# Window attention in three parts a step, values in two passes, and accumulating transfers for the low parts of weights

## The chip, the cores and the metric

The kernel runs on one core of a Trainium2 chip. The metric is the device time of one execution in microseconds (us); the number reported is the median of several runs. The engines are TensorE (PE; its weight loads are PEld), VectorE (DVE), ScalarE (ACT), GpSimd (POOL) and SyncE (SP, which issues the transfers). L172 is line 172 of the kernel before.

## The reference

Two layers of a hybrid block on a sequence of 512 tokens of width 1024 (a convolution branch, a retention branch and a window attention branch, each gated, summed and projected), and then one layer of a second block (a spatial gate, a gated linear recurrence, a feed-forward part). All in float32. What the change touches is the window attention of the first block, run once in each of the two layers:

```
q, k, v = h @ w_in (16 heads of 64; 4 key/value heads of 64, each used by 4 heads)
q, k    = rms_norm over 64, rotary on 16 of the 64
for each block n of 128 queries: keys of blocks n-1, n, n+1 (2 blocks at the ends)
    s = q k^T / 8, masked to |i - j| <= 128
    m = max(max(s), sink);  p = exp(s - m) / (sum(exp(s - m)) + exp(sink - m))
    o = p v
y_attn = (o * silu(gate)) @ w_attn_out
```

## The kernel before, in words

**Products in three passes.** A float32 product is made of three passes of TensorE over operands split into a high part (rounded to the format fp32r) and a low part (the value less its high part): high x high, high x low, low x high (`mm3`, L170 to L174). `fm` makes one 128 x 512 product tile from 8 blocks of weights of 128 x 128, so 24 passes of 512 columns, in one of two PSUM banks of the pool `mm`. `tm` makes four tiles at a time in the four banks of the pool `acc`. A third pool, `misc`, has two banks.

**Weights.** All weights come as chunks of 8 blocks (128 x 1024, 512 KB) in the order of their use. SP loads a chunk into one of three `raw` tiles; `_split_next` (L132) makes `hi` on ACT (L149) and `lo = raw - hi` on DVE (L150), in three tiles each (WB = 3). `take` (L155) splits chunk c + 2 when chunk c is first used.

**Attention.** `att_kv` makes keys and values, `att_q` the queries of a group of 8 heads, `att_gate` the gates (4 products per group); `att_kT` and `att_qT` transpose keys and queries through `att_T` (4 transposes L673 and a split). `att_core` (L739) runs over a group g of 8 heads: 8 steps (4 blocks n of 128 queries, 2 sets of 4 heads), as a pipeline over three steps. At step `it` it gives out, in this order: the value products of step it - 2 (`mm3` into a `misc` bank, 2 or 3 key blocks of 3 passes each; then 4 DVE operations on 64 partitions), the transposes of the probabilities of step it - 1 (4 for each key block, L771, each key block in a `misc` bank and then split by ACT L205 and DVE L206), and the scores of step `it` (12 matmuls, L792, contracting over 64 partitions, 256 or 384 columns wide) with mask, maximum (L794), exponentials (L223) and scaling. The two halves of the partitions hold two different key/value heads. Then it yields.

**Order.** `weave` gives out one unit of dense products and one step of the attention by turns: the convolution's input products (`conv_ab`, 8 units of one `fm` per group) beside `att_core`. A scheduler puts the instructions of each engine in a fixed order before the run, by order of issue and by when it reckons them ready; an `issue_after` block ties an instruction behind another on its engine. In the second group the convolution's taps (`conv_taps`, 30 DVE operations for each of 8 tiles) run in the background, some for each dense unit (`bg_rate`).

`layer` (L829) calls, per layer: keys and values; `att_q` of group 0; its gates; `conv_ab` 0 to 3 woven with `att_core` 0; `att_q` of group 1; its gates; `conv_ab` 4 to 7 woven with `att_core` 1; then `branch_out` (8 pairs of a gate product and an output product).

Of the kernel before, what the change touches and what calls it, by code (L numbers as in the profile page):

```python
# [10 lines left out]
F32 = mybir.dt.float32  # L11
# [56 lines left out]
class Kern:  # L68
    def __init__(self, ctx, tc, ap):
        self.tc, self.nc, self.ap = tc, tc.nc, ap  # L70
        nc = self.nc
        self.V, self.A, self.T = nc.vector, nc.scalar, nc.tensor
        pool = lambda n, b, **k: ctx.enter_context(tc.tile_pool(name=n, bufs=b, **k))
        self.cp = pool("cp", 1)
        self.sp = pool("sp", NSLOT)
        self.rp = pool("rp", WB)
        self.hp = pool("hp", WB)
        self.lp = pool("lp", WB)
        self.ep = pool("ep", 2)
# [11 lines left out]
        self.first = {}  # L91
        self.bg = None
        self.bg_rate = self.credit = 0
# [38 lines left out]
    def _split_next(self):  # L132
        c = self.nsplit
        if c >= NCHUNK:
            return
        while self.nraw <= c:
            self._load_raw()
        raw = self.raw.pop(c)
        if c in HOLD:
            parts = [self.split(raw[:, i * 512:i * 512 + 512]) for i in range(2)]  # L140
            self.hi[c], self.lo[c] = [x[0] for x in parts], [x[1] for x in parts]
        else:
            h = self.hp.tile([128, 1024], F32R, tag="hi", name=f"hi{c}")
            l = self.lp.tile([128, 1024], F32R, tag="lo", name=f"lo{c}")
            if c in self.first:
                with self.tc.issue_after(self.first[c].ins):
                    self.A.copy(h, raw)  # L147
            else:
                self.A.copy(h, raw)  # L149
            self.V.tensor_tensor(out=l, in0=raw, in1=h.bitcast(F32), op=ALU.subtract)  # L150
            self.hi[c], self.lo[c] = h, l
        self.nsplit += 1
        self._load_raw()

    def take(self, key, rows, cols, n=128):  # L155
# [12 lines left out]
        return h[:, o * 128:o * 128 + n], l[:, o * 128:o * 128 + n]  # L168

    def mm3(self, out, lh, ll, rh, rl, start, stop):  # L170
        T = self.T
        T.matmul(out, lhsT=lh, rhs=rh, start=start, stop=False)  # L172
        T.matmul(out, lhsT=lh, rhs=rl, start=False, stop=False)  # L173
        T.matmul(out, lhsT=ll, rhs=rh, start=False, stop=stop)  # L174

    def fm(self, key, cols, rhs, blocks=None, ts=None, pool=None):
# [239 lines left out]

    def conv_ab(self, l, ms):
        for m in ms:
            pb = self.fm(("w_in", l), O_GLU + D + m * 128, self.h)
            t = self.slot()  # L420
            self.act(t, pb, AF.Tanh, scale=0.5)
            yield
            pa = self.fm(("w_in", l), O_GLU + m * 128, self.h)
            v = self.slot()
# [245 lines left out]
    def att_T(self, xs, p):  # L670
# [3 lines left out]
        return self.split(ps)  # L674

    def att_kv(self, l, xg, xs):
        for ps in self.tm(("w_in", l), O_AK, xg):
            if ps is None:
                yield
        self.rms_h(xs, self.vk("norm_g", l), range(KT // 2))  # L680
        self.av = []
        for i in range(2):
            h, lo = self.slot(F32R), self.slot(F32R)
            for j in range(2):
                t = 2 * i + j
                c = slice(j * 256, j * 256 + 256)
                r = self.r[:, t:t + 1]
                self.act(h[:, c], ps[t][:, 256:512], AF.Copy, scale=r)
                self.stt(lo[:, c], ps[t][:, 256:512], r, h[:, c].bitcast(F32), ALU.mult, ALU.subtract)
            self.av.append((h, lo))  # L690
        ks = []
# [47 lines left out]
    def att_core(self, l, g):  # L739


        T = self.T
        qT, kT, av, sg = self.qT, self.kT[g], self.av, self.asg
        by_b = lambda x: x.rearrange("q (b p) -> q b p", b=2)
        sink, nsink = (by_b(x[:, 8 * g:8 * g + 8]) for x in (self.vk("sink", l), self.nsink))
        ya = [self.slot() for _ in range(4)]
        iters = [(n, pp) for n in range(NT) for pp in range(2)]
        hss = [slice(0, 64), slice(64, 128)]
        s1, s2 = {}, {}
        for it in range(len(iters) + 2):  # L750
            if 0 <= it - 2:
                n, pp = iters[it - 2]
                pt = s2.pop(it - 2)
                ps = self.misc()
                for x, (jb, ph, pl) in enumerate(pt):
                    c = (jb % 2) * 256 + g * 128
                    vh, vl = av[jb // 2]
                    self.mm3(ps, vh[:, c:c + 128], vl[:, c:c + 128], ph, pl, x == 0, x == len(pt) - 1)
                ns = slice(n * 128, n * 128 + 128)
# [3 lines left out]
            if 0 <= it - 1 < len(iters):  # L763
                n, pp = iters[it - 1]
                pr = s1.pop(it - 1)
                j0 = max(0, n - 1)
                pt = []
                for x in range(min(NT, n + 2) - j0):
                    ps = self.misc()
                    for i in range(4):  # L770
                        T.transpose(ps[:, i * 128:i * 128 + 128], pr[i][:, x * 128:x * 128 + 128], self.ck("ident"))  # L771
                    h, lo = self.split(ps)
                    pt.append((j0 + x, h, lo))
                s2[it - 1] = pt
            if it < len(iters):
                n, pp = iters[it]
                j0, j1 = max(0, n - 1) * 128, min(NT, n + 2) * 128
# [4 lines left out]
                rs = self.small([128, 4], tag="rs")  # L782
                ns = slice(n * 128, n * 128 + 128)
                sps = [None] * 4
                for x in range(2):
                    qh, ql = qT[2 * pp + x]
                    kh, kl = kT
# [9 lines left out]
                of = slice(2 * pp, 2 * pp + 2)  # L797
                nm = self.small([128, 4], tag="nm")
                self.stt(by_b(nm), by_b(rm), -0.125, nsink[:, :, of], ALU.mult, ALU.min)
                es = self.small([128, 4], tag="es")  # L800
                self.tt(by_b(es), sink[:, :, of], by_b(nm), ALU.add)
                pr = [self.slot() for _ in range(4)]
# [11 lines left out]
                s1[it] = pr  # L814
            yield
        self.ya += [self.split(y) for y in ya]

# [11 lines left out]
    def layer(self, l, xs, acc, xg):  # L829
# [41 lines left out]
        self.weave(self.conv_ab(l, range(4, 8)), self.att_core(l, 1))  # L871
        self.kT = self.av = self.qT = self.asg = None
        self.bg_rate = RATES[1]
        ys, self.ya = self.ya, None
        self.go(self.branch_out(l, 2, ("ao", l), ys))
        ys = None
        self.bg_rate = RATES[2]
# [675 lines left out]
```

## Time and profile before

| | |
|---|---|
| Runs | 3067.52 us median of 3 (3067.11 to 3069.32) |
| The profiled execution | 3067.16 us, span 3065.4 us |
| PE / PEld / DVE / ACT busy share of the span | 99% / 81% / 68% / 37% |
| Chain of work that ended last, by engine | PE 90%, DVE 7%, ACT 2%, issue 1%, DMA 1% |
| Mean DMA rate | 94 GB/s |

A row of "busy" gives the duration of instructions; matmuls are pipelined, so the time that one takes of TensorE is read from the starts of two that follow each other in the timeline, not from its duration. The four passes through `att_core` lie at about 90 to 172, 219 to 302, 1104 to 1188 and 1233 to 1318 us.

### The profile page before, as it was taken

Reading aid. Unit: us, or ns where it says so; the run is one execution under the profiler, and the core shown is the slowest. Engines: PE = TensorE matmul, PEld = TensorE weight load, DVE = VectorE, ACT = ScalarE, POOL = GpSimd, SP = SyncE. Lnnn points to the kernel's source line nnn. Section 1 sums busy time; section 2 is a strip of 40 time slices with the busy share of each in tenths; the row PEclk is TensorE's granted clock in tenths of the full one; section 3 lists DMA queues with packets and bytes.
Section 4 is the critical chain, followed back from the end, with each engine's and each line's share of the span. In section 5 each row is a group of like instructions: output and inputs, shape, how many; then the busy total and the mean of one; then the engine's idle time right before and its main releaser. Section 6 shows DMA issues by size and latency. Waiting matters only on the chain.

```text
span 3065.4 us, 36069 instructions
## 1 busy us (share of the span) xinstructions
PE 3022.8 (99%) x13996; PEld 2470.4 (81%) x13996; DVE 2078.2 (68%) x3787; ACT 1130.5 (37%) x1783; POOL 0.2 (0%) x4
## 2 busy tenths in 40 slices
PE   8999999999999999999999999999999999999998
PEld 6777888887888877788888788887888888788887
DVE  7778897877444776889787764467776754753326
ACT  4545223334233444532333433333543332422222
POOL 0000000000000000000000000000000000000000
PEclk9999999999999999999999999999999999999999
DMA  4121322221233321122222132254222223422234
GB/s 163 63 69 49 97 89 76 83 76 63 95 98 129 117 76 62 62 83 97 71 74 76 63 103 96 97 173 143 90 90 69 65 74 123 161 96 99 98 110 151
DMA packets 83980, 288.99 MB, mean 94 GB/s; under 512 B 9440, under 2 KB 9696, under 8 KB 83680
## 3 DMA queue, kind: packets, MB, share of 16 engines
q1 hardware_dynamic: 83808, 286.68, 28.3%
q8 instruction: 110, 1.80, 0.2%
q14 instruction: 62, 0.51, 0.1%
HBM read 282.45 MB, written 4.19 MB: 94 GB/s over the span
## 4 chain that ended last, share of the span: by engine, by line
PE 90%; DVE 7%; ACT 2%; issue 1%; DMA 1%; SPq 0%; DVEq 0%; ACTq 0%
PE pm L172 20%; PE pm L174 20%; PE pm L173 20%; PE pa L172 6%; PE pa L174 6%; PE pa L173 6%; DVE lo L150 1%; DVE s L213 1%; PE pi L771 1%; PE pa L792 1%; PE pi L172 1%; DVE s L210 1%; PE pi L174 1%; PE pi L173 1%; ACT s L223 1%
## 5 line engine op out<-in xcount | busy, mean ns | idle before, releaser
L172 PE MATMUL pm<-s,hi 128*128 128x512 f32 x2848 | 1115.1, 392 | 1.9 <-ACT hi L149 1.2
L173 PE MATMUL pm<-s,hi 128*128 128x512 f32 x2848 | 1113.9, 391 | 0.0
L174 PE MATMUL pm<-s,lo 128*128 128x512 f32 x2848 | 1110.7, 390 | 0.5 <-DVE lo L150 0.5
L149 ACT CAST hi<-raw 128x1024 fp32r<-128x1024 f32 x497 | 523.2, 1053 | 1394.4 <-PE pm L173 761.2
L150 DVE TENSOR_TENSOR lo<-raw,hi 128x1024 fp32r<-128x1024 f32 x500 | 610.1, 1220 | 491.0 <-ACT hi L149 485.4
L172 PEld LDWEIGHTS pm<-s,hi 128*128 128x128 f32 x2848 | 534.5, 188 | 117.1 <-issue 3.5
L174 PEld LDWEIGHTS pm<-s,lo 128*128 128x128 f32 x2848 | 534.7, 188 | 113.1 <-issue 2.2
L173 PEld LDWEIGHTS pm<-s,hi 128*128 128x128 f32 x2848 | 534.8, 188 | 110.1 <-issue 1.7
L213 DVE SCALAR_TENSOR_TENSOR s<-s,m,s 128x497 f32<-128x497 f32 (+10 forms) x528 | 390.2, 742 | 11.4
L172 PE MATMUL pa<-hi,s 128*128 128x512 f32 x830 | 329.2, 397 | 9.3 <-ACT hi L147 6.7
L173 PE MATMUL pa<-lo,s 128*128 128x512 f32 x830 | 326.9, 394 | 4.8 <-DVE lo L150 4.8
L174 PE MATMUL pa<-hi,s 128*128 128x512 f32 x830 | 325.6, 393 | 0.0
L213 DVE SCALAR_TENSOR_TENSOR s<-s,pm 128x512 f32<-128x512 f32 x164 | 112.0, 683 | 147.4 <-PE pm L174 147.0
L172 PEld LDWEIGHTS pa<-hi,s 128*128 128x128 f32 x830 | 156.8, 189 | 43.0 <-ACT hi L147 6.7
L173 PEld LDWEIGHTS pa<-lo,s 128*128 128x128 f32 x830 | 157.1, 189 | 38.3 <-DVE lo L150 7.5
L174 PEld LDWEIGHTS pa<-hi,s 128*128 128x128 f32 x830 | 156.8, 189 | 31.8
L205 ACT CAST s<-s 128x512 fp32r<-128x512 f32 x184 | 110.4, 621 | 178.8 <-DVE s L213 139.1
L206 DVE TENSOR_TENSOR s<-s,s 128x512 fp32r<-128x512 f32 x184 | 123.0, 687 | 29.0 <-ACT s L205 28.2
L210 DVE TENSOR_TENSOR s<-s,s 128x512 f32<-128x512 f32 (+2 forms) x178 | 114.1, 662 | 1.7
L223 ACT ACTIVATE s<-s 128x512 f32<-128x512 f32 (+1 forms) x130 | 79.4, 628 | 89.9 <-DVE s L210 25.2
L223 ACT ACTIVATE s<-pa,m 128x256 f32<-128x256 f32 (+2 forms) x136 | 69.3, 524 | 77.4 <-DVE m L213 74.7
L213 DVE SCALAR_TENSOR_TENSOR s<-s,s 128x512 f32<-128x512 f32 (+1 forms) x130 | 88.1, 685 | 7.8 <-ACT s L223 6.3
(155 smaller groups left out, 2376.2 us busy)
## 6 DMA issues: line engine op xcount, KB each, us to landing
raw<-w SPq DMA_DIRECT2D x509, 512.0 KB, 3.3
s<-xT SPq DMA_DIRECT2D x16, 256.0 KB, 5.4
xd<-s SPq DMA_DIRECT2D x8, 256.0 KB, 2.0
s<-xd SPq DMA_DIRECT2D x8, 256.0 KB, 5.7
out<-s SPq DMA_DIRECT2D x8, 256.0 KB, 2.8
s<-c_ln_g SPq DMA_DIRECT2D x6, 256.0 KB, 4.4
s<-c_ln_b SPq DMA_DIRECT2D x6, 256.0 KB, 4.9
ckt<-ck SPq DMA_DIRECT2D x1, 1344.0 KB, 6.3
```

Of the source, the lines that this page charges most:

```text
L149: self.A.copy(h, raw)
L150: self.V.tensor_tensor(out=l, in0=raw, in1=h.bitcast(F32), op=ALU.subtract)
L172: T.matmul(out, lhsT=lh, rhs=rh, start=start, stop=False)
L173: T.matmul(out, lhsT=lh, rhs=rl, start=False, stop=False)
L174: T.matmul(out, lhsT=ll, rhs=rh, start=False, stop=stop)
L205: self.A.copy(h, src)
L206: self.V.tensor_tensor(out=l, in0=src, in1=h.bitcast(F32), op=ALU.subtract)
L210: return self.V.tensor_tensor(out=out, in0=a, in1=b, op=op)
L213: return self.V.scalar_tensor_tensor(out=out, in0=a, scalar=s, in1=b, op0=op0, op1=op1)
L223: return self.A.activation(out, a, f, bias=bias, scale=scale, **kw)
L771: T.transpose(ps[:, i * 128:i * 128 + 128], pr[i][:, x * 128:x * 128 + 128], self.ck("ident"))
L792: T.matmul(ps[:, 0:w], lhsT=a[hs, ns], rhs=b[hs, j0:j1], start=first, stop=last)
```

## The change

- `att_core` is cut into three parts per step, with a yield behind each: scores of step `it` and the transposes of the first two key blocks of step it - 1; the transposes of the third key block, where there is one; the values of step it - 2.
- `conv_ab` goes through `fm_parts`, which yields inside a product: the 8 blocks of one product come in three parts (cuts before blocks 3 and 5 in group 0, 2 and 5 in group 1), so that dense parts and attention parts alternate.
- `behind` ties the scores behind the last dense pass and the last value pass that were given out, and the transposes and the next dense part behind the last score matmul.
- Each score matmul pair now works on one key/value head: `twice` copies every key head next to itself (8 ACT copies), 4 `att_T` instead of 2 transpose them, and the reordering of the heads in the weights goes.
- The value tile holds high and low part of a head side by side, 64 columns each, and is the stationary operand: two passes (probabilities high and low) instead of three give both halves on 64 partitions each, in a bank of the pool `mm` instead of `misc`. Two ACT copies across partitions and two DVE additions put the halves together; two DVE operations on 128 partitions apply the gate instead of four on 64.
- From the second gate product of group 0 to the first unit of `branch_out`, the low part of a weight chunk is made by ACT (`l = -raw`, rounded) and a transfer issued by POOL that adds `raw` to it, instead of by DVE.
- `att_q` of group 1 is woven with the end of `att_core` 0; in group 1 the last gate product and `branch_out` are woven with `att_core` 1, whose first part is given out ahead.

```diff
@@ _split_next
+            added = self.added and c not in self.first
+            if added:
+                self.act(l, raw, AF.Copy, scale=-1.0)
+                self.nc.gpsimd.dma_start(out=l, in_=raw, accum_op=ALU.add)
...
-            self.V.tensor_tensor(out=l, in0=raw, in1=h.bitcast(F32), op=ALU.subtract)
+            if not added:
+                self.V.tensor_tensor(out=l, in0=raw, in1=h.bitcast(F32), op=ALU.subtract)
@@ new
+    @contextmanager
+    def behind(self, on=True):
+        with ExitStack() as c:
+            for x in self.pe if on else ():
+                c.enter_context(self.tc.issue_after(x.ins))
+            yield
+    def fm_parts(self, key, cols, rhs, cuts):
+        ps = self.mm()
+        for k, (rh, rl) in enumerate(rhs):
+            if k in cuts:
+                yield
+            wh, wl = self.take(key, 128 * k, cols)
+            with self.behind(k == 0 or k in cuts):
+                self.mm3(ps, wh, wl, rh, rl, k == 0, k == len(rhs) - 1)
+        return ps
+    def twice(self, xs):
+        out = []
+        for x in xs:
+            y = self.slot()
+            yr, xr = y.rearrange("p (h x d) -> p h x d", x=2, d=64), x[:, 0:256].rearrange("p (h d) -> p h d", d=64)
+            for i in range(2):
+                self.A.copy(yr[:, :, i, :], xr)
+            out.append(y)
+        return out
@@ att_kT
-        self.kT = []
-        for p in range(2):
+        ks, self.kT = self.twice(ks), []
+        for p in range(4):
@@ att_core, scores
+                self.pe = (self.dense, *self.pv) if it > 0 else ()
...
-                            T.matmul(ps[:, 0:w], lhsT=a[hs, ns], rhs=b[hs, j0:j1], start=first, stop=last)
+                            with self.behind():
+                                scored = T.matmul(ps[:, 0:w], lhsT=a[hs, ns], rhs=b[hs, j0:j1], start=first, stop=last)
+                            if it > 0:
+                                self.pe = (scored,)
@@ att_core, transposes (turned(x) as before, each with self.behind())
+                turned(0)
+                turned(1)
+                s2[it - 1] = pt
+            if it <= len(iters):
+                yield
+            if 0 < it <= len(iters) and len(blocks) > 2:
+                turned(2)
+            if it < len(iters):
+                yield
@@ att_core, values
-                    self.mm3(ps, vh[:, c:c + 128], vl[:, c:c + 128], ph, pl, x == 0, x == len(pt) - 1)
-                for i in range(4):
-                    hs, p = hss[i // 2], 2 * pp + i % 2
-                    self.stt(ya[p][hs, ns], sg[p][hs, ns], 0.5, ps[hs, i * 128:i * 128 + 128], ALU.mult, ALU.mult)
+                ps = self.mm()
+                for x, (jb, ph, pl) in enumerate(pt):
+                    v = av[jb][:, c:c + 128]
+                    T.matmul(ps, lhsT=v, rhs=ph, start=x == 0, stop=False)
+                    self.pv = [T.matmul(ps, lhsT=v, rhs=pl, start=False, stop=x == len(pt) - 1)]
+                y = self.slot()
+                for u in range(2):
+                    cs, o = slice(u * 256, u * 256 + 256), hss[1 - u]
+                    self.A.copy(y[hss[u], 0:256], ps[o, cs])
+                    self.tt(y[hss[u], 0:256], y[hss[u], 0:256], ps[hss[u], cs], ALU.add)
+                for x in range(2):
+                    p = 2 * kv + x
+                    self.stt(ya[p][:, ns], sg[p][:, ns], 0.5, y[:, x * 128:x * 128 + 128], ALU.mult, ALU.mult)
@@ layer
+        self.added = True
...
-        self.weave(self.conv_ab(l, range(0, 4)), self.att_core(l, 0))
-        self.go(self.att_q(l, 1))
+        self.weave(chain(self.conv_ab(l, range(0, 4), (3, 5)), self.att_q(l, 1)), self.att_core(l, 0))
...
-        self.weave(self.att_gate(l, 1), qpost, 1)
-        self.weave(self.conv_ab(l, range(4, 8)), self.att_core(l, 1))
+        self.weave(self.att_gate(l, 1, range(3)), qpost, 1)
+        core = self.att_core(l, 1)
+        next(core)
+        def dense():
+            self.bg_rate = RATES[0] / 3
+            yield from self.att_gate(l, 1, range(3, 4))
+            yield from self.conv_ab(l, range(4, 8), (2, 5))
+            for i, _ in enumerate(self.branch_out(l, 2, ("ao", l), self.ya)):
+                yield
+                self.bg_rate = RATES[1]
+                if i == 0:
+                    self.added = False
+        self.weave(dense(), core)
```

## Rows read from the trace of the kernel before

**Rows 1.** The page, busy time by engine over the span.

```profile
PE 3022.8 (99%) x13996; PEld 2470.4 (81%) x13996; DVE 2078.2 (68%) x3787; ACT 1130.5 (37%) x1783; POOL 0.2 (0%) x4
```

**Rows 2.** Windows, one step: us; PE, PEld, DVE, ACT, POOL busy; clock; DMA; GB/s.

```profile
126.91:137.93 11.02, 11.00 (x58) 8.39 (x56) 8.26 (x22) 6.57 (x16) 0.00 (x0) 1.00 0.13 48
```

**Rows 3.** Timeline of PE, that step: start us, us, instructions.

```profile
126.91 0.60 PE L771 MATMUL pi<-ckt,s 128*128 128x128 f32 x4
...
128.25 0.63 PE L771 MATMUL pi<-ckt,s 128*128 128x128 f32 x4
128.80 0.96 PE L792 MATMUL pa<-s,s 64*128 64x384 f32 x7
129.70 0.49 PE L172 MATMUL pm<-s,hi 128*128 128x512 f32 x1
130.13 0.66 PE L771 MATMUL pi<-ckt,s 128*128 128x128 f32 x4
130.54 0.47 PE L173 MATMUL pm<-s,hi 128*128 128x512 f32 x1
...
135.88 0.39 PE L172 MATMUL pi<-s,s 128*128 128x512 f32 x1
...
138.02 0.62 PE L792 MATMUL pa<-s,s 64*128 64x384 f32 x4
```

**Rows 4.** Timeline of PE, a step at the last query block, its attention part.

```profile
149.51 0.60 PE L771 MATMUL pi<-ckt,s 128*128 128x128 f32 x4
...
152.73 0.50 PE L172 MATMUL pm<-s,hi 128*128 128x512 f32 x1
```

**Rows 5.** Timeline of PE, the end of the first pass.

```profile
164.05 0.40 PE L174 MATMUL pi<-s,s 128*128 128x512 f32 x1
165.49 0.50 PE L172 MATMUL pa<-hi,s 128*128 128x512 f32 x1 [1.04 <-ACT s L223]
```

**Rows 6.** Timeline of PE, transposes and scores each between dense passes.

```profile
86.39 1.03 PE L673 MATMUL pi<-ckt,s 128*128 128x128 f32 x8
87.18 0.48 PE L172 MATMUL pm<-s,hi 128*128 128x512 f32 x1
87.50 0.40 PE L173 MATMUL pm<-s,hi 128*128 128x512 f32 x1
...
89.77 0.39 PE L174 MATMUL pm<-s,lo 128*128 128x512 f32 x1
90.09 0.97 PE L792 MATMUL pa<-s,s 64*128 64x256 f32 x12
90.99 0.50 PE L172 MATMUL pm<-s,hi 128*128 128x512 f32 x1
91.33 0.40 PE L173 MATMUL pm<-s,hi 128*128 128x512 f32 x1
```

**Rows 7.** Groups over the span: line, engine, shapes, count, busy us, mean ns, waits.

```profile
L149 ACT CAST hi<-raw 128x1024 fp32r<-128x1024 f32 x497 | 523.2, 1053 | 1394.4 <-PE pm L173 761.2 <-issue 345.2 <-PE pa L174 202.0
L150 DVE TENSOR_TENSOR lo<-raw,hi 128x1024 fp32r<-128x1024 f32 x500 | 610.1, 1220 | 491.0 <-ACT hi L149 485.4 <-PE pi L980 1.6 <-ACT hi L147 1.2
L213 DVE SCALAR_TENSOR_TENSOR s<-s,pi 64x128 f32<-64x128 f32 x128 | 31.5, 282 | 4.6 <-PE pi L174 4.0
L210 DVE TENSOR_TENSOR s<-s,m 128x256 f32<-128x256 f32 x40 | 15.2, 416 | 0.2
L217 DVE TENSOR_SCALAR s<-s,m 128x384 f32<-128x384 f32 x32 | 11.9, 415 | 0.3
L223 ACT ACTIVATE s<-pa 128x256 f32<-128x256 f32 x8 | 2.6, 382 | 0.0
L213 DVE SCALAR_TENSOR_TENSOR s<-s,pm 128x512 f32<-128x512 f32 x164 | 112.0, 683 | 147.4 <-PE pm L174 147.0
```

**Rows 8.** Issues of transfers: count, KB each, median us from issue to landing.

```profile
raw<-w SPq DMA_DIRECT2D x509, 512.0 KB, 3.3
s<-c_ln_b SPq DMA_DIRECT2D x6, 256.0 KB, 4.9
```

More of the change, by code (lines that the diff above doesn't have):

```diff
@@ L1 @@
 import math
-from contextlib import ExitStack
+from contextlib import ExitStack, contextmanager
+from itertools import chain
 import numpy as np
@@ L173, in mm3 @@
         T.matmul(out, lhsT=lh, rhs=rl, start=False, stop=False)
-        T.matmul(out, lhsT=ll, rhs=rh, start=False, stop=stop)
+        self.dense = T.matmul(out, lhsT=ll, rhs=rh, start=False, stop=stop)
     def fm(self, key, cols, rhs, blocks=None, ts=None, pool=None):
@@ L414, in weave, with conv_ab @@
                     cl = False
-    def conv_ab(self, l, ms):
+    def conv_ab(self, l, ms, cuts):
         for m in ms:
-            pb = self.fm(("w_in", l), O_GLU + D + m * 128, self.h)
+            pb = yield from self.fm_parts(("w_in", l), O_GLU + D + m * 128, self.h, cuts)
             t = self.slot()
@@ L422, in conv_ab @@
             yield
-            pa = self.fm(("w_in", l), O_GLU + m * 128, self.h)
+            pa = yield from self.fm_parts(("w_in", l), O_GLU + m * 128, self.h, cuts)
             v = self.slot()
@@ L681, in att_kv @@
         self.av = []
[L682 to L690, printed above, removed]
+        for t in range(NT):
+            v, r = self.slot(F32R), self.r[:, t:t + 1]
+            vr = v.rearrange("p (h x d) -> p h x d", x=2, d=64)
+            pv = ps[t][:, 256:512].rearrange("p (h d) -> p h d", d=64)
+            self.act(vr[:, :, 0, :], pv, AF.Copy, scale=r)
+            self.stt(vr[:, :, 1, :], pv, r, vr[:, :, 0, :].bitcast(F32), ALU.mult, ALU.subtract)
+            self.av.append(v)
         ks = []
@@ L742, in att_core @@
         T = self.T
-        qT, kT, av, sg = self.qT, self.kT[g], self.av, self.asg
-        by_b = lambda x: x.rearrange("q (b p) -> q b p", b=2)
-        sink, nsink = (by_b(x[:, 8 * g:8 * g + 8]) for x in (self.vk("sink", l), self.nsink))
+        qT, av, sg = self.qT, self.av, self.asg
         ya = [self.slot() for _ in range(4)]
-        iters = [(n, pp) for n in range(NT) for pp in range(2)]
+        iters = [(n, kv) for n in range(NT) for kv in range(2)]
         hss = [slice(0, 64), slice(64, 128)]
@@ L750, in att_core @@
         for it in range(len(iters) + 2):
[L751 to L757, printed above, removed]
-                    self.mm3(ps, vh[:, c:c + 128], vl[:, c:c + 128], ph, pl, x == 0, x == len(pt) - 1)
-                ns = slice(n * 128, n * 128 + 128)
-                for i in range(4):
-                    hs, p = hss[i // 2], 2 * pp + i % 2
-                    self.stt(ya[p][hs, ns], sg[p][hs, ns], 0.5, ps[hs, i * 128:i * 128 + 128], ALU.mult, ALU.mult)
[L763 to L774, printed above, removed]
             if it < len(iters):
-                n, pp = iters[it]
+                n, kv = iters[it]
                 j0, j1 = max(0, n - 1) * 128, min(NT, n + 2) * 128
@@ L796, in att_core @@
                                                     accum_out=rm[:, i:i + 1])
-                of = slice(2 * pp, 2 * pp + 2)
+                o = 8 * g + 4 * kv
+                sink, nsink = (x[:, o:o + 4].rearrange("q (p u) -> q u p", u=2) for x in (self.vk("sink", l), self.nsink))
+                by_u = lambda x: x.rearrange("q (u p) -> q u p", u=2)
                 nm = self.small([128, 4], tag="nm")
-                self.stt(by_b(nm), by_b(rm), -0.125, nsink[:, :, of], ALU.mult, ALU.min)
+                self.stt(by_u(nm), by_u(rm), -0.125, nsink, ALU.mult, ALU.min)
                 es = self.small([128, 4], tag="es")
-                self.tt(by_b(es), sink[:, :, of], by_b(nm), ALU.add)
+                self.tt(by_u(es), sink, by_u(nm), ALU.add)
                 pr = [self.slot() for _ in range(4)]
@@ L814, in att_core, with turned @@
                 s1[it] = pr
+            if 0 < it <= len(iters):
+                n = iters[it - 1][0]
+                pr, pt = s1.pop(it - 1), []
+                blocks = list(range(max(0, n - 1), min(NT, n + 2)))
+                def turned(x):
+                    ps = self.misc()
+                    for i in range(4):
+                        with self.behind():
+                            T.transpose(ps[:, i * 128:i * 128 + 128], pr[i][:, x * 128:x * 128 + 128], self.ck("ident"))
+                    pt.append((blocks[x], *self.split(ps)))
+                turned(0)
[5 more added lines that the diff above has]
+                turned(2)
+            pr = pt = turned = None
+            if it < len(iters):
+                yield
+            if 0 <= it - 2:
+                n, kv = iters[it - 2]
+                pt = s2.pop(it - 2)
+                ns = slice(n * 128, n * 128 + 128)
+                c = (2 * g + kv) * 128
+                ps = self.mm()
[11 more added lines that the diff above has]
+                    self.stt(ya[p][:, ns], sg[p][:, ns], 0.5, y[:, x * 128:x * 128 + 128], ALU.mult, ALU.mult)
+                pt = None
+            if it > len(iters):
+                qT = av = sg = None
+                self.pe = ()
+                self.ya += [self.split(y) for y in ya]
             yield
-        self.ya += [self.split(y) for y in ya]
     def load_rest(self):
@@ L1534 @@
             mats[n, l] = x[n][l]
-        order = np.array([8 * g + 4 * (i % 2) + i // 2 for g in range(2) for i in range(8)])
-        idx = (order[:, None] * 64 + np.arange(64)[None, :]).reshape(-1)
-        mats["aq", l] = x["w_in"][l][:, O_AQ + idx]
-        mats["ag", l] = x["w_in"][l][:, O_AG + idx]
-        mats["ao", l] = x["w_attn_out"][l][idx]
+        mats["aq", l] = x["w_in"][l][:, O_AQ:O_AQ + D]
+        mats["ag", l] = x["w_in"][l][:, O_AG:O_AG + D]
+        mats["ao", l] = x["w_attn_out"][l]
     for n in ("w_in_2", "w_a_2", "w_b_2", "w_o_2", "w_ffn_gate_2", "w_ffn_up_2", "w_ffn_down_2", "w_ple_2",
```

13 lines of the change are left out of this document (6 added, 7 removed).

## Prediction

> **What bounds the kernel now.** I read the page's busy times first: TensorE is busy for 99% of the span, DVE for 68%, ACT for 37% [rows 1]. So the time is TensorE's own row of passes, and a change counts by the passes that it takes out or puts in and by the holes that it closes or opens. The windows of one middle step of the attention show the same in small: 11.02 us, TensorE busy throughout at full granted clock (1.00, so 2.4 GHz), DVE 8.26, ACT 6.57 [rows 2]. Busy hides small holes, since the durations overlap, so the third view is the timeline, read from start to start. The nine value passes of that step start at 135.88 and the next group starts at 138.02; with 0.09 us for the switch (below) a pass of 512 columns takes (2.14 - 0.09) / 9 = 0.228 us [rows 3]. A product of 24 passes is 5.46 us, the pace of one weight chunk.
>
> The same view gives the floors of the small work. Eight transposes run from 86.39 to 87.18, 0.099 us each; twelve scores of 256 columns take 0.90 us, 0.075 each [rows 6]; seven of 384 columns take 0.90, 0.128 each [rows 3]. A switch costs: 89.77 to 90.09 is 0.32 against 0.23, so 0.09 us into scores; 0.34 and 0.32 behind scores and transposes, so 0.11 and 0.09 out of them [rows 6].
>
> **The change, part by part.**
>
> *Values.* 2 + 3 + 3 + 2 key blocks for two sets of heads are 20 per pass through the attention, 80 over two groups and two layers. Each loses one pass of three: 80 x 0.228 = 18.2 us off TensorE. Nothing else has to run in their place, so this is the firm term.
>
> *Holes in the attention steps.* In the middle step the transposes and scores stand from 126.91 to 130.54 with one dense pass (0.23) among them: 3.40 us [rows 3]. The floor is 12 x 0.099 + 12 x 0.128 = 2.73; four switches of the new order (into scores, scores to transposes, twice out of transposes) add 0.36: 3.09 if nothing waits, 0.3 less. Three of eight steps are like it. At the last block the part takes 149.51 to 152.73, 3.22 + 0.11 for the way out [rows 4], against 1.19 + 0.90 + 0.36 = 2.45: 0.9 less. The cause is that the scores wait for freed `acc` banks and the transposes for `misc` banks that values hold too, with nothing dense between them. The change puts dense parts there and takes the values out of `misc`. The four other steps have fewer blocks; I put them at 0.2, between nothing and 0.9. So 0.9 + 0.9 + 0.8 = 2.6 us per pass, 10.4 for four. Bounds: nothing, if the waits move, and 0.9 x 32 = 28.8.
>
> *End of group 0.* `att_q` waits for exponentials to free its banks: 164.05 to 165.49, 1.44 against 0.23 [rows 5], once in each layer, 2.4 together. The weave puts other parts there, but `att_q`'s first pass still needs the same four banks, 5 us of parts behind the last scores. I take half, 1.2; bounds 0 and 2.4.
>
> *The bank shared with dense products.* New and not shown: `mm` has two banks; with values in one, each product must wait until the product before it has been read out, with only the value passes as cover (6 or 4 passes, 1.37 or 0.91 us). The read of a dense bank is 0.68 us on DVE [rows 7], and from the start of the last pass about 0.4 more until it can begin: 1.1, against 0.23 + 0.91 = 1.14 or 0.23 + 1.37 = 1.60. It just fits if the reading engine is free. In the middle step ACT would be busy 6.57 + 1.05 (negation) + 2 x 0.38 (copies) = 8.4 of some 10 us; DVE 8.26 - 1.22 - 4 x 0.28 + 2 x 0.42 + 2 x 0.28 = 7.3 [rows 2, 7]. An engine busy four fifths of the time makes the read wait for part of an instruction of 0.4 to 1.2 us. I take 0.3 us for each of the 24 steps with values followed by a product, 7.2 in all; bounds 0 and 1.2 (one chunk operation in front each time), 29.
>
> *Keys twice.* 2 more `att_T` per layer: 16 transposes x 0.099 = 1.6 us. The eight ACT copies (0.38 each [rows 7]) follow the rotation tile by tile; only the last pair can stand on the path: 0.4 per layer, 0.8; bounds 0 and 2 x 8 x 0.38 = 6.1.
>
> *Low parts by transfer.* DVE loses 1.22 us per chunk, ACT gains 1.05 [rows 7], both beside TensorE. The transfer's latency X is not shown: POOL has 0.2 us of work in the whole span [rows 1]. Bounds by the nearest rows: a plain load of the same 512 KB lands in 3.3 us; an addition reads two tiles and writes one, so twice that is 6.6, and the longest of the small loads on the shared queue take 4.9 [rows 8]; for the upper end I allow three times 6.6, 20. I take 6.6, to which the rows are nearest; below nothing the edit can't come here, since TensorE is busy for 11.00 of the 11.02 us and so waits for no low part [rows 2]. What it must meet: a `lo` tile is filled two chunks ahead and read for one, so three chunks of 5.46 us hold ACT's operations (1.05 and about half a us of waiting), X and the reading (5.46): X up to 9.4 us costs nothing even in the dense stretches, in the attention steps of 10 us up to 18. Behind the negation on ACT's queue stand the exponentials, so a late `raw` would stop these too; `raw` has three chunks less 1.05 and the load of 3.3, 11 us or more. The engines of the queue are 13% busy in that step [rows 2]. Cost zero at 6.6, with ACT's and TensorE's other work as cover; beyond 9.4 each us costs a third of a us on some 20 dense chunks (queries and gates, both layers), 6.7 us in all.
>
> The SBUF page of the Trainium skill ("SBUF — State Buffer", section "SBUF: two separate sides") speaks against this edit: a transfer issued from POOL has its descriptors written by POOL's cores, and these are shut out while VectorE runs in its two-port mode. No run here shows it. By that rule the two scalings of a step, 0.415 us each [rows 7], would lengthen X by up to 0.8 us, to 7.4, still under 9.4; it would matter for the second rival only.
>
> *Sum.* -18.2 - 10.4 - 1.2 + 7.2 + 1.6 + 0.8 = -20.2. The profiled execution took 3067.16 us, 0.36 under the median of 3067.52, so 3047.0 for it and 3047 for the median, a span of about 3045.
>
> **The rivals.**
>
> *The bank hand-over takes the gain.* For: ACT at 8.4 of 10 us, its exponentials in a row of more than 2 us, and a fixed order on each engine. Against: the read is given out before the values. At 1.2 us per hand-over 28.8 in place of 7.2: 3047 + 21.6 = 3069, no change. It decides at 1.14 us per step.
>
> *The accumulating transfer is late.* This is the one that ends slower. At X = 15 us the dense chunks cost (15 - 9.4) x 6.7 = 37 us: 3084. It is slower than before from X = 9.4 + 20.5 / 6.7 = 12.5 us on. For: two reads and one write, an issuer that no row shows, a single queue in order. Against: 12.5 is almost four times the plain load of the same tile [rows 8], and the engines are mostly free.
>
> *All holes close.* The parts and their ties work as drawn, the hand-over is free and the few-block steps gain 0.5 each: 18.2 + 1.8 x 4 + 0.5 x 16 + 2.4 - 1.6 = 34.2, so 3033. For: DVE and `misc` are relieved at once. Against: ACT's load rises just there.
>
> *It does not act*: the scheduler's fixed order leaves holes of the same sum elsewhere and only the passes go: 18.2 - 9.6 = 8.6, 3059, or with switches at each cut a little above.
>
> **How the numbers follow.** Forecast 0.48, its own range 3037 to 3056; hand-over 0.15; late transfer 0.15; all holes 0.15; passes only 0.07. A difference under 0.2% (6 us) can't be told from none. Faster (under 3061.4): 0.48 + 0.15 + 0.06 + a quarter of the hand-over case 0.04 = 0.73. Same (to 3073.7): 0.09 of the hand-over case and 0.02 of the late transfer = 0.11. Slower: the rest of these two, 0.02 + 0.13, and 0.01 of the last = 0.16. The range 3031 to 3078 leaves a tenth above (transfers later than X = 14) and some 0.06 below.
>
> **What would show it.** Right: 160 value passes of 512 columns in `pm` banks instead of 240 in `pi`; middle steps of about 10 us from scores to scores; DVE's L150 down by some 60 instructions; TensorE still the chain's 90%. The hand-over shows as a hole ahead of a product's first pass, released by ACT or DVE reading `pm`. Late transfers show as TensorE or ACT released by a DMA on `lo` or `raw` in the query and gate stretches, and an issue-to-landing time over 9 us. Wrong would be: steps of 11 us or more, or holes in the stretches of queries and gates.

## The result and the profile after

The kernel after takes 3118.72 us in the median (3114.3 to 3121.03, 4 runs) beside 3068.42 for the kernel before in the same session: ratio 1.0162, 95% interval 1.0145 to 1.018. It is slower by 50 us; 3047 was forecast, 71.7 us less, and the range ended at 3078.

The page of the kernel after, busy time by engine, answers to [rows 1]. Its chain that ended last shows by engine who set the end.

```profile
PE 3028.7 (97%) x13932; PEld 2473.1 (79%) x13932; DVE 2024.1 (65%) x3727; ACT 1213.1 (39%) x1931; POOL 55.4 (2%) x68
...
PE 86%; DVE 7%; ACT 5%; issue 1%; DMA 0%; SPq 0%; DVEq 0%; ACTq 0%
```

The work went as counted: 80 value passes out and 16 transposes in make 64 matmuls fewer (13996 to 13932). Yet TensorE's share falls from 99 to 97% of a longer span, and ACT's share of the chain rises from 2 to 5%.

The waits of TensorE in the kernel after (engine, line, what it waited for: us in total, times, longest), the rows on the banks of the dense products (`pm`):

```profile
PE pm L190 <- ACT s L252: 14.7, 9, 2.6
PE pm L864 <- DVE s L242: 10.5, 5, 3.3
PE pm L190 <- DVE s L242: 9.1, 4, 2.4
...
PE pm L864 <- ACT s L252: 6.2, 4, 2.0
```

L190 is the first pass of a dense product, L864 the first value pass. L252 and L242 are lines of helpers, through which ACT and DVE read a dense product out of its bank (L252 is also the line of ACT's scalings and negations). Together 40.5 us; in the kernel before no row on `pm` is above 1.2 us.

The windows of the kernel after, four whole middle steps from scores to scores, answer to [rows 2] (columns as there):

```profile
105.97:119.07 13.10, 10.53 (x51) 8.11 (x50) 6.57 (x21) 8.57 (x20) 1.72 (x2) 0.87 0.60 144
119.07:133.79 14.72, 11.49 (x53) 8.55 (x52) 7.50 (x22) 7.63 (x18) 0.86 (x1) 0.83 0.32 75
133.79:148.43 14.64, 12.06 (x55) 9.11 (x55) 6.90 (x21) 8.13 (x19) 0.86 (x1) 0.85 0.28 69
148.43:163.25 14.82, 12.04 (x55) 9.18 (x55) 7.49 (x22) 7.63 (x18) 0.86 (x1) 0.85 0.30 72
```

13 to 15 us a step in place of 11 to 12 before and the "about 10" of the forecast, TensorE idle for 2.6 to 3.2 us in each, and a mean granted clock of 0.83 to 0.87. No engine is full: ACT, the busier of the two others, has 8.57 of 13.10. Steps of 11 us or more were what the prediction had named as a sign of being wrong.

The timeline of the kernel after, the hole of the first of these steps (start us, us, engine, line, instruction; idle time and releaser in brackets):

```profile
111.37 0.39 PE L192 MATMUL pm<-s,lo 128*128 128x512 f32 x1
...
111.53 0.60 ACT L234 CAST s<-pi 128x512 fp32r<-128x512 f32 x1
111.60 0.39 PE L864 MATMUL pm<-s,s 128*128 128x512 f32 x1
...
112.15 1.12 ACT L252 ACTIVATE s<-s,m 128x384 f32<-128x384 f32 x2
112.28 0.39 PE L865 MATMUL pm<-s,s 128*128 128x512 f32 x1
...
113.18 0.56 ACT L234 CAST s<-pi 128x512 fp32r<-128x512 f32 x1
113.64 1.06 ACT L252 ACTIVATE lo<-raw 128x1024 fp32r<-128x1024 f32 x1
...
114.60 0.58 ACT L252 ACTIVATE s<-pm 128x512 f32<-128x512 f32 x1
...
115.24 0.79 PE L190 MATMUL pm<-s,hi 128*128 128x512 f32 x1 [2.57 <-ACT s L252]
```

The last dense pass starts at 111.37, four value passes fill the other bank, and then TensorE stands: the next product needs the bank that ACT reads out at 114.60, 3.2 us after that pass. ACT is never idle in between. It casts, scales two rows, casts again and negates a weight chunk, all of which its fixed order puts ahead of the read-out. In the step after it the reader is DVE, whose read-out at 128.92 stands behind the split of a third key block, and that waits for a cast behind ACT's negation; the hole ends at 129.65:

```profile
126.75 1.05 ACT L252 ACTIVATE lo<-raw 128x1024 fp32r<-128x1024 f32 x1
...
127.71 0.57 ACT L234 CAST s<-pi 128x512 fp32r<-128x512 f32 x1
...
128.31 0.69 DVE L235 TENSOR_TENSOR s<-pi,s 128x512 fp32r<-128x512 f32 x1 [0.74 <-ACT s L234]
128.92 0.68 DVE L242 SCALAR_TENSOR_TENSOR s<-s,pm 128x512 f32<-128x512 f32 x1
```

The windows of that second hole and of the stretch behind it:

```profile
125.61:129.65 4.04, 0.82 (x5) 0.42 (x4) 2.91 (x6) 3.99 (x7) 0.86 (x1) 0.90 0.07 14
129.65:133.79 4.14, 4.14 (x9) 2.81 (x9) 1.33 (x4) 0.36 (x1) 0.00 (x0) 0.50 0.68 123
```

In the hole TensorE works for 0.82 of 4.04 us. Behind it the granted clock is 0.50, the 1.2 GHz level, for the whole of 4.14 us, in which nine passes run; at the 0.228 us of [rows 3] they would take 2.05. So the hole costs another 2.1 us after it has ended.

An account for layer 1, worked out from the starts in the timeline: over the two passes of the attention, the distance from start to start less the floor of the work between (0.227 us for a pass, 0.099, 0.128 and 0.0755 for the small work of [rows 3, 6]) sums to 18.2 us lost before and 51.3 after, of which 6.8 in 34 dense passes of about 0.42 us. The scores, transposes and value passes that started at the lower clock lost about 6 more, so the clock took some 13 us in this layer, and some 10 in layer 2. (These are estimates from the starts in the timeline: for each instruction of TensorE that started while the granted clock was 0.50, the distance to the next start less the floor, counted up to the floor itself.) Twice the difference, less 18.2 for the values, plus the 2.4 forecast for the keys, is 50.4; the runs showed 50.3. The time is in the attention, and it is all there, apart from the 2.4 us that are the forecast's own.

### The profile page after: what moved, and what is told of

The parts are those of the page before. It is cut to its first block, busy times and chain, and to the rows that moved or that the text cites. A ratio compares the mean times of both kernels' runs of the same rounds, so it can differ in the third digit from the quotient of the medians.

```text
span 3119.3 us, 36159 instructions
## 1 busy us (share of the span) xinstructions
PE 3028.7 (97%) x13932; PEld 2473.1 (79%) x13932; DVE 2024.1 (65%) x3727; ACT 1213.1 (39%) x1931; POOL 55.4 (2%) x68
## 4 chain that ended last, share of the span: by engine, by line
PE 86%; DVE 7%; ACT 5%; issue 1%; DMA 0%; SPq 0%; DVEq 0%; ACTq 0%
PE pm L190 20%; PE pm L191 19%; PE pm L192 19%; PE pa L190 7%; PE pa L191 7%; PE pa L192 7%; ACT s L252 3%; DVE s L242 2%; DVE s L239 1%; DVE pa L812 1%; PE pa L808 1%; ACT s L234 1%; PE pa L1144 1%; DVE lo L159 1%; ACT hi L157 1%
## 5 line engine op out<-in xcount | busy, mean ns | idle before, releaser
L190 PE MATMUL pm<-s,hi 128*128 128x512 f32 x2848 | 1125.6, 395 | 25.0 <-ACT s L252 14.7
L159 DVE TENSOR_TENSOR lo<-raw,hi 128x1024 fp32r<-128x1024 f32 x436 | 532.6, 1222 | 496.6 <-ACT hi L157 493.1
L190 PEld LDWEIGHTS pm<-s,hi 128*128 128x128 f32 x2848 | 537.7, 189 | 140.7 <-ACT s L252 18.3
L242 DVE SCALAR_TENSOR_TENSOR s<-s,m,s 128x497 f32<-128x497 f32 (+10 forms) x528 | 390.9, 744 | 11.3
L190 PE MATMUL pa<-hi,s 128*128 128x512 f32 x830 | 331.1, 400 | 6.9 <-ACT hi L155 6.6
L242 DVE SCALAR_TENSOR_TENSOR s<-s,pm 128x512 f32<-128x512 f32 x164 | 112.0, 683 | 143.3 <-PE pm L192 134.0
L190 PEld LDWEIGHTS pa<-hi,s 128*128 128x128 f32 x830 | 157.9, 190 | 40.2 <-ACT hi L155 6.6
L235 DVE TENSOR_TENSOR s<-s,s 128x512 fp32r<-128x512 f32 x184 | 123.3, 689 | 30.3 <-ACT s L234 29.2
L239 DVE TENSOR_TENSOR s<-s,pm 64x256 f32<-64x256 f32 (+1 forms) x88 | 43.2, 492 | 117.6 <-PE pm L192 59.5
L252 ACT ACTIVATE s<-s 128x512 f32<-128x512 f32 (+1 forms) x130 | 79.1, 627 | 94.4 <-DVE s L239 28.9
L242 DVE SCALAR_TENSOR_TENSOR s<-s,s 128x512 f32<-128x512 f32 (+2 forms) x194 | 104.1, 556 | 8.1 <-ACT s L252 6.2
```

The source lines that it names most:

```text
L235: self.V.tensor_tensor(out=l, in0=src, in1=h.bitcast(F32), op=ALU.subtract)
L239: return self.V.tensor_tensor(out=out, in0=a, in1=b, op=op)
L242: return self.V.scalar_tensor_tensor(out=out, in0=a, scalar=s, in1=b, op0=op0, op1=op1)
L252: return self.A.activation(out, a, f, bias=bias, scale=scale, **kw)
```

## The experiments

Three theories. **A**: the value products take a dense bank, and the next product waits for a late read-out. **B**: ACT's chain is too long by the negation. **C**: the ties hold back from TensorE what could run in the hole (the next scores, whose operands are ready).

**Values in a bank of the transposes**

```diff
@@ att_core of the kernel after
-                ps = self.mm()
+                ps = self.misc()
```

> The changed kernel, with the value products back in a misc bank (two passes, three parts, ties and transfers stay). Theory A, the hand-over: the holes of 2 to 3 us ahead of the next dense or value passes come from the shared pair of mm banks, so they go and with them the half clock behind them: 3040 to 3075 us. Theory B, the longer chain on ACT (negation, copies) makes every step late whatever bank is used: 3105 to 3125. Theory C, the fixed order keeps dense work out of the holes: also 3105 or more.

3074.63 us, ratio to before 1.0024 (1.0015 to 1.0034): 44 us less than after. The waits on `pm` are gone from the list; the largest that came is on the values' own bank, by the split that last read it:

```profile
PE pi L864 <- DVE s L235: 12.3, 15, 1.6
```

**No accumulating transfers**

```diff
@@ layer of the kernel after
-        self.added = True
+        self.added = False
```

> The changed kernel, with the low parts of all weights made on DVE as before (no negation on ACT, no accumulating transfer). Theory A: the read-out of the dense bank stands about 1 us less late behind ACT, so the holes shrink by some 0.5 to 1 us in 24 steps: 3085 to 3110. Theory B: the holes were the negation's, so they go: 3075 or less. Theory C: no change, 3115 and up.

3128.33 us, ratio 1.0199 (1.018 to 1.0218). Without the negation on ACT the time is 9.6 us longer, with intervals that just touch, and in the range that C had named. The same read-outs are late, up to 4.2 us:

```profile
PE pm L190 <- ACT s L252: 14.3, 9, 4.2
PE pm L864 <- DVE s L242: 12.1, 6, 3.3
PE pm L190 <- DVE s L242: 12.0, 4, 3.1
```

B falls as a cause by itself: the negation is one of the instructions ahead of the read-out, but with it goes the relief of DVE, whose subtractions are back (L159 x500), and the sum is no better. What the negation costs apart from that relief, this run can't tell.

**No ties**

```diff
@@ behind
-            for x in self.pe if on else ():
+            for x in ():
```

> The changed kernel without the ties between scores, transposes and dense parts on TensorE (each may be put anywhere). Theory A: the bank still hands over late, 3100 to 3125. Theory C: the order was the cause, 3075 or less.

3062.34 us, ratio 0.9984 (0.9975 to 0.9994): 56 us less than after, with the shared bank left in. A had expected 3100 or more here, and C 3105 or more with the bank of the transposes; each removal takes most of the price away. So neither A nor C alone makes the hole.

**Before with the two passes alone** (keys twice and values in two passes in `misc`, the old uncut steps, no transfers)

```diff
@@ att_core of the kernel before
-                    self.mm3(ps, vh[:, c:c + 128], vl[:, c:c + 128], ph, pl, x == 0, x == len(pt) - 1)
+                    v = av[jb][:, c:c + 128]
+                    T.matmul(ps, lhsT=v, rhs=ph, start=x == 0, stop=False)
+                    T.matmul(ps, lhsT=v, rhs=pl, start=False, stop=x == len(pt) - 1)
```

> The kernel before with only the two-pass values (keys twice, high and low part of values side by side), still in a misc bank, steps uncut, no transfer. By the prediction's terms 18.2 us of passes go, 1.6 to 2.4 come for the keys: 3050 to 3054. If the four more operations on ACT and DVE per step are what costs, 3068 or more.

3067.25 us, ratio 1.0000 (0.9991 to 1.0009). It lies in neither of the two ranges expected, just under the second. The firm 18.2 us bring nothing here. The account of lost time in layer 1 rises from 18.2 to 25.6; the timeline of this kernel shows a place, between scores and transposes:

```profile
108.71 1.34 PE L806 MATMUL pa<-s,s 64*128 64x384 f32 x12
111.22 0.63 PE L785 MATMUL pi<-ckt,s 128*128 128x128 f32 x4 [1.17 <-DVE s L210]
```

**Three banks for dense products and values, one for the rest**

```diff
-        self.mmp = pool("mmp", 2, space=PSUM)
+        self.mmp = pool("mmp", 3, space=PSUM)
...
-        self.mip = pool("mip", 2, space=PSUM)
+        self.mip = pool("mip", 1, space=PSUM)
```

> Kernel after with three banks for the dense products and values and one for the rest (transposes, turned queries), ties kept. If the wait for a bank of the dense products is what stops TensorE (theory A), the holes ahead of L190 that end with ACT s L252 or DVE s L242 go and the time falls to about 3075, as with the values outside these banks; one bank for the transposes gives some of it back (up to 1 us in each of 32 steps, so 3075 to 3105). If it is not the number of banks but that the values stand in the written order between dense parts (theory C), the time stays at 3110 or above.

3076.54 us, ratio 1.0029 (1.0017 to 1.0041). Order and ties as after; one bank more takes away 42 us. In its timeline the next product starts right behind the values:

```profile
110.39 0.39 PE L865 MATMUL pm<-s,s 128*128 128x512 f32 x1
110.62 0.39 PE L190 MATMUL pm<-s,hi 128*128 128x512 f32 x1
```

**Scores free of the last products**

```diff
@@ att_core of the kernel after
-                self.pe = (self.dense, *self.pv) if it > 0 else ()
+                self.pe = ()
```

> Kernel after in which the scores of a step are no longer tied behind the last dense product and the last value product; transposes and dense parts stay tied behind the scores. Theory C in its narrow form (the hole is there because the next scores, whose operands are ready, may not enter it): scores stand ahead of L190 in the holes and the time falls to 3070 or below. Theory A alone (a bank that comes free late stops the queue whatever stands in it): scores stay where they are or only move the hole, 3105 to 3120.

3058.98 us, ratio 0.9973 (0.9962 to 0.9984), 60 us less than after. This run shows the mechanism best, because ACT's order in the step is the same. Its timeline:

```profile
108.80 0.39 PE L192 MATMUL pm<-s,lo 128*128 128x512 f32 x1
...
109.58 1.12 ACT L252 ACTIVATE s<-s,m 128x384 f32<-128x384 f32 x2
...
110.03 1.32 PE L808 MATMUL pa<-s,s 64*128 64x384 f32 x11
...
110.61 0.56 ACT L234 CAST s<-pi 128x512 fp32r<-128x512 f32 x1
111.08 1.06 ACT L252 ACTIVATE lo<-raw 128x1024 fp32r<-128x1024 f32 x1
112.03 0.58 ACT L252 ACTIVATE s<-pm 128x512 f32<-128x512 f32 x1
...
112.67 0.50 PE L190 MATMUL pm<-s,hi 128*128 128x512 f32 x1 [1.32 <-ACT s L252]
```

The read-out starts 3.2 us after the start of the last dense pass, as late as in the kernel after. But eleven of the scores now stand in the hole, 1.32 us of it are left in place of 2.57, and behind it the clock stays up (windows of this run):

```profile
112.67:116.16 3.49, 3.49 (x19) 2.65 (x19) 2.85 (x11) 1.66 (x3) 0.62 (x1) 1.00 0.73 140
```

**Both: values in a bank of the transposes, no ties**

> Kernel after without any tie and with the values in a bank of the transposes. If bank and ties are two halves of one cause (the hole needs both), the second removal brings little over the first: 3055 to 3065. If each costs by itself, the two add: 3067 - (3119 - 3075) - (3119 - 3062) + 52 lies near 3018; below 3045 says that.

3053.11 us, ratio 0.9952 (0.9937 to 0.9967). The four kernels of bank and ties side by side:

```
                      ties      no ties
shared bank          3118.7     3062.3
own bank             3074.6     3053.1
```

The bank costs 44 us with the ties and 9 without, the ties 56 with the shared bank and 22 without: two halves of one cause (35 us come only where both are there), each with a price of its own, 9 and 22. The time is 2 us under the range expected for two halves and far above the 3018 expected for two separate costs.

**No ties and no transfers** (the edits of the second and third run together)

> Kernel after without ties and without the accumulating transfer (the lower parts of all weights by VectorE's subtraction). With ties the transfer was worth 9.6 us (3128.3 against 3118.7). If that worth comes from holes in which VectorE's queue stands behind splits of weights, it shrinks with the holes: 3062 to 3067 (0 to 5 us above the kernel without ties). If VectorE's 64 subtractions a run are time by themselves, it stays 9 to 10 us: 3071 to 3073.

3076.19 us, ratio 1.0029 (1.0019 to 1.0038): the transfers are worth 13.9 us here. I had tied their worth to the holes, expecting 0 to 5, or 9 to 10 if it were DVE's time alone; it is above both. In the run without ties and with transfers, TensorE's transposes waited for DVE's splits (L235) as in the first row; without transfers, as in the second:

```profile
PE pi L844 <- DVE s L235: 1.5, 6, 0.3
```

```profile
PE pi L844 <- DVE s L235: 12.2, 18, 1.5
```

**Before with the transfers alone**

```diff
@@ _split_next and layer of the kernel before: as in the kernel after
+                self.act(l, raw, AF.Copy, scale=-1.0)
+                self.nc.gpsimd.dma_start(out=l, in_=raw, accum_op=ALU.add)
```

> Kernel before with nothing but the accumulating transfers for the lower parts of the weights while attention runs (negation on ScalarE, transfer issued by GpSimd, no subtraction on VectorE). The prediction put this part at 0. With the new steps it was worth 9.6 us (ties) and 14 us (no ties). If that worth hangs on the new steps, whose holes end with VectorE, it is 0 to 3 us here (3064 to 3068). If the 32 subtractions of a layer, 1.22 us each, stand ahead of attention's own work on VectorE's queue in the old steps too, it is 6 to 12 us (3055 to 3061).

3064.3 us, ratio 0.9991 (0.9982 to 1.0): about 3 us, hardly to be told from none. The worth hangs on the new steps.

**Passes and transfers, steps uncut** (the two runs on the kernel before together)

> Kernel before with values in two passes in a bank of the transposes, keys twice, and the accumulating transfers; steps uncut and in the old order. Passes alone gave 3067.3, the transfers gave 10 to 14 us where VectorE's queue was late. If both are terms that add: 3053 to 3058, and cutting the steps in three adds nothing to speak of (the cut kernel without ties is at 3053.1). If the cut steps are needed to turn fewer passes into time: 3060 to 3067.

3066.76 us, ratio 0.9995 (0.9985 to 1.0004). The terms don't add; without the cuts neither is turned into time.

**Values in a bank of the transposes, scores free, other ties kept**

> Kernel after with the values in a bank of the transposes and the scores free of the last products; the other ties (transposes and dense parts behind the scores) kept. The two halves of the cause are gone, so it lies with the kernel without any tie (3053.1) or, as with the shared bank (3059.0 against 3062.3), some 3 us under it: 3047 to 3055. Above 3060 would say that the ties that are left cost by themselves once the bank is free.

3056.29 us, ratio 0.9968 (0.9955 to 0.998), beside 0.9952 (0.9937 to 0.9967) with no tie at all. It is 1 us above the range expected. The intervals overlap: what the other ties cost once the scores are free can't be told from nothing.

**Old neighbours** (on the kernel of 3053.1: `att_q` of group 1, the fourth gate product and `branch_out` back where the kernel before has them; steps stay cut)

```diff
-        self.weave(chain(self.conv_ab(l, range(0, 4), (3, 5)), self.att_q(l, 1)), self.att_core(l, 0))
+        self.weave(self.conv_ab(l, range(0, 4), (3, 5)), self.att_core(l, 0))
+        self.go(self.att_q(l, 1))
...
-        self.weave(dense(), core)
+        self.weave(self.conv_ab(l, range(4, 8), (2, 5)), self.att_core(l, 1))
```

> Kernel after without ties and with the values in a bank of the transposes (3053.1), and in it the neighbours of attention put back where they stood before: the queries of group 1 after the first pass, the fourth gate product before the second, the output product after it. The steps stay cut in three. Between it and the uncut kernel with passes and transfers (3066.8) lie the cuts, between it and 3053.1 the woven neighbours. If the cuts turn the fewer passes into time: 3053 to 3058 (the prediction gave the ends of the passes 1.2). If the woven neighbours do: 3062 to 3067.

3088.86 us, ratio 1.0073 (1.0057 to 1.009), and no answer: the edit also dropped the line that paces the convolution's taps per part, so three parts of a product pulled three times as many. The attention's steps were not slower. A large loss lay 600 us later, in the retention; the windows:

```profile
720.00:740.00 20.00, 10.95 (x31) 5.87 (x30) 11.59 (x27) 8.96 (x15) 0.00 (x0) 0.61 0.08 27
```

**Old neighbours, the pace set right**

```diff
+        self.bg_rate = RATES[0] / 3
         self.weave(self.conv_ab(l, range(4, 8), (2, 5)), self.att_core(l, 1))
```

> The kernel of the run before (old neighbours, cut steps, no ties, values in a bank of the transposes) with the depthwise taps paced per part as in the kernel after (a third of the rate while the products are cut); the run before had left the rate of whole products on parts three times as many, and its 36 us were lost at 720 to 760 us, in the retention, not in attention, whose steps were as quick as in the kernel at 3053.1. If that is the whole of the 36 us: 3053 to 3058, and the cuts bring the gain. If the woven neighbours bring it: 3062 to 3067. If taps and retention are still out of step: above 3070.

3048.78 us, ratio 0.9933 (0.9916 to 0.9949): 20.5 us under before, the best of all, and 4 us under the lowest range expected. The retention's stretch is full again, and the step shown takes 9.57 us (windows of this run):

```profile
123.96:133.53 9.57, 9.41 (x49) 6.92 (x48) 6.23 (x21) 6.06 (x16) 0.86 (x1) 1.00 0.45 110
...
720.00:740.00 20.00, 20.00 (x95) 16.32 (x94) 17.24 (x27) 12.02 (x20) 0.00 (x0) 1.00 0.17 57
```

That step has only eight transposes and four value passes in it, so it is not yet the "about 10" of the forecast. A fair measure is three steps together, with 36 scores, 36 transposes and 72 dense passes. In this run they go from the first of these rows to the second:

```profile
114.78 1.32 PE L808 MATMUL pa<-s,s 64*128 64x384 f32 x12
...
146.35 0.97 PE L808 MATMUL pa<-s,s 64*128 64x256 f32 x12
```

In the kernel before they go from this row to the first of [rows 4], at 149.51:

```profile
115.41 0.96 PE L792 MATMUL pa<-s,s 64*128 64x384 f32 x7
```

They take 31.57 us with 16 value passes here and 34.10 with 27 before. Eleven passes of 0.228 us are 2.51 of the 2.53 between them: the best kernel gains its passes, and closes hardly any hole.

From the uncut kernel with passes and transfers (3066.8) the cuts bring 18 us. Weaving the neighbours in brought nothing. That it cost 4 us is not shown by the times, whose intervals overlap; the account below, 18.8 beside 17.0 a layer, points the same way.

The account of lost time closes within 3.2 us for the seven kernels below. Layer 1, us, and what twice its rise over 18.2 gives with -18.2 for the values and +2.4 for the keys, beside the difference measured:

```
                                         lost   worked out   measured
after                                    51.3      +50.4       +50.3
values in a bank of the transposes       28.6       +5.0        +7.3
no ties                                  22.0       -8.2        -5.0
two passes alone, uncut                  25.6       -1.0        -0.1
two passes and transfers, uncut          24.3       -3.6        -0.8
own bank, no ties                        18.8      -14.6       -14.6
the same, old neighbours, pace right     17.0      -18.2       -20.5
```

## Why the prediction was wrong

**The bank shared with dense products** is the step that failed. The term was 0.3 us for each of 24 steps, 7.2, with 29 as its upper end. The trace of after shows 40.5 us of waits on `pm`, in pieces of up to 3.3 us, and by the estimate above some 23 us at the lower clock, most of it behind such waits. That is 56 us over the term, more than three quarters of the 71.7 missed. The step argued by load: "An engine busy four fifths of the time makes the read wait for part of an instruction". The load itself was right, 8.4 us of ACT in a step against 7.6 to 8.6 in the four windows. What decides is not a share but the place of the read-out in a fixed queue: two casts, two scalings and a negation of ACT stood ahead of it, in the step of the timeline above. (No run moved the read-out alone in that queue; that its place sets the wait is read from the timelines, and that the wait makes the loss is shown by the runs with a bank more and with free scores.) The upper end allowed for one chunk operation in front. The against-argument of the rival, that the read is given out before the values, says nothing about the engine that reads. The rival had the mechanism and stopped at 3069, since its price was capped at 1.2 us a step and the fall of the clock behind a hole had no term.

**Holes in the attention steps** came to nothing in place of -10.4, by the account: 51.3 less 20.2 of hand-over waits and 13 at the lower clock is 18.1 in layer 1, beside 18.2 before. With the 56 that makes some 67 of the 71.7. I took the ties as the drawing of a good order; they also forbid, and 22 us come back without them even where the bank is not shared. Without ties and sharing the term is still hardly a gain: 17.0 to 18.8 against 18.2. The cuts keep the holes from growing by 6 to 7 us a layer, as they do uncut, and close next to none.

**Values**: 18.2 us did leave TensorE, but "the firm term" was firm only if nothing else was late; uncut, new holes ate nearly all of it. **Low parts by transfer** was put at zero and turned out a gain. The landing time is 4.6 us in the kernel after, under the 6.6 taken and the 9.4 allowed, so the late transfer was no danger (the page's issues of transfers, columns as in [rows 8]):

```profile
raw<-w SPq DMA_DIRECT2D x509, 512.0 KB, 3.3
lo<-raw POOLq DMA_DIRECT2D x64, 512.0 KB, 4.6
```

and taking 64 operations of 1.22 us off DVE's queue was worth 10 to 14 us in the cut steps and 3 or less in the old ones. I had asked only whether TensorE waits for a low part, not what stands behind DVE's subtraction in its queue. The longest of the 256 KB loads on the page of before take 5.7 us, not the 4.9 that the prediction read, which changes nothing in its 6.6; and the first transfer of the kernel after is issued at 48.8 us, among the queries of group 0, ahead of its second gate product. Whether DVE's port mode holds up the issue, as the Trainium skill ("SBUF — State Buffer", section "SBUF: two separate sides") has it, no run here shows apart. **End of group 0**: no wait of `att_q` for exponentials is left in the list of after (2.1 us in two waits before), but the weave can't be credited: with the old neighbours and cut steps, where `att_q` follows the pass again, none is left either. In the kernel after the scores wait anew at the start of group 1 (`pa` L808, 3.1 us in two waits). **Keys twice** is not contradicted: with its 2.4 the account closes within 3.2 us in every kernel of the table.

The direction of the forecast was that of the parts without their two conditions: the same parts without the sharing, the ties and the woven neighbours give 3048.8. That this is near the 3047 forecast is luck: there the holes gained 2.4 us in place of 10.4 (17.0 a layer beside 18.2), and no hand-over had to be paid with 7.2.

## What to carry to other kernels

Before two uses share a double-buffered bank, find the instruction that frees it and list what stands ahead of it in its engine's queue; the wait is the sum of these, not the engine's load. An order forced with ties is safe only where the tied engine can't stall: leave free at least one piece of work whose operands are ready. And a hole on TensorE can cost more than itself: here the lower clock added some 23 us to 40.5 of waits.

## What the runs showed of the hardware

In the kernel after, the granted clock fell to 0.50, the 1.2 GHz level, about the ends of the four holes of 2.2 to 2.6 us before 115.24, 129.65, 145.03 and 159.41, with passes of about 0.42 us behind them. It also fell behind two shorter holes, of 1.55 us before 236.99 and of 1.09 before 271.43, but not behind one of 1.51 before 172.61, nor behind the one of 1.32 us in the run with free scores. So the length of one hole did not settle whether the clock fell.

An addition by transfer of 512 KB within the core's memory landed in 4.6 us beside 3.3 for a plain load of the same size, with DVE busy 65% of the span, and in 5.0 where nothing else of the kernel before was changed.
